# Attention prologue: where the second step's scores are issued

## The chip, the cores and the metric

The kernel runs on one NeuronCore of one Trainium2 chip. The metric is the device time of one execution in microseconds, as the median of several executions. The profile shows the engines of this core: PE (TensorE matmul) with PEld (its weight loads), DVE (VectorE), ACT (ScalarE), POOL (GpSimd) and SP (SyncE, which issues most transfers here).

## What is computed

The reference runs two trunk layers on 1024 latent tokens and 128 context tokens of width 1024, in float32. Layer 0 projects the normalised tokens into a convolution path, a neighbourhood-attention path (8 heads of 64) and a SiLU gate for each. Layer 1 is a pooling mixer. Only the end of layer 0's projections and the start of its attention matter here:

```
a, b, ga, q, k, v, gb = split(h @ w_in)
z_conv = conformer_conv(a, b) * silu(ga)
s = concat(q @ k_window.T * scale + bias, q @ k_ctx.T * scale)
p = softmax(s)
z_att = (p @ concat(v_window, v_ctx)) * silu(gb)
x = x + gate * (concat(z_conv, z_att) @ w_out)
```

## The kernel before

**Projections.** Tokens lie in three groups of 384 (index `g`; the third holds 256 latent and 128 context tokens). A projection is a chain of 24 matmuls into one PSUM bank (`chain_ws`, line 230): eight slices of the inner dimension, with three products each, since each float32 operand is split into a high and a low part. The matmuls of slices 0 to 3 read the first pair of weight tiles, those of slices 4 to 7 the second.

The last projection is `p_ga` (line 764): for each group four chains, `i` = 0 to 3. Chains 0 and 1 read the weights `W0`, chains 2 and 3 read `W1`. Behind each chain stand a Tanh on ACT (line 535) and a product on DVE (line 536, these two are `silu2`), which free the chain's bank, and a second product on DVE (line 774). Below, "chain 0" to "chain 3" are those of the third group, `g` = 2; chain 3 is the last projection chain of the layer.

**Attention.** It runs in 16 steps (`STEPS`, line 1044). Step s is a triple of head pair, half of the grid rows and first column block; steps 0 and 1 share the head pair and the half. The work of one step:

- `scores` (line 939): for each of two column blocks (`matmuls(i)`), six matmuls into two PSUM banks (line 954), then two DVE instructions (line 959) that add the bias, write the tile `p` and take the row extremum. With that four banks are written and four line 959 instructions issued per step. `exp` (line 966): four Exp on ACT with row sums. `norm` (line 968): a reciprocal on DVE and two scalings on POOL (line 972) per column block.
- `turn` (line 976): four groups of four transposes of `p` into banks, which ACT (lines 1137 and 1143) and DVE (line 1144) copy out to `pt`.
- `values` (line 981): 32 matmuls of `pt` with the values, in the step after.

`attention_steps` runs these as a pipeline: in iteration s it issues the scores of step s + 1, the values of step s - 1, the turns of step s, and a part of `prep` (line 875), which turns the queries and keys of the next head pair, or of `prompt_attention`. In iteration 0 the part of `prep` is the two `q_half` calls (transposes at line 891, an ACT copy at line 882 and a DVE subtraction at line 883 each).

`first_scores` (line 1059) issues the scores, exps and norms of step 0 from inside `p_ga`, after chain 2. `attention_ahead(1)` (line 1046), behind the second group, issues the whole `prep` of head pair 0, the second half's bias loads and the values' loads.

**What sets the order.** `attention` wraps its steps in `manual_schedule` (line 1073) for PE, ACT and DVE: there each of the three engines takes these instructions in the order of the program text. For everything else a planner fixes every engine's order ahead of the run, in a time of its own. At each point it takes, of the instructions whose inputs and buffers are there, the one that stands first in the program text. An instruction of `attention` stands behind all of `p_ga` in the text. The finished order is static: on the chip each engine's list is worked off as it stands, each instruction with its waits.

**Buffers that the steps share.**

- PSUM: the tag `mm` has four banks, used by the chains and by the scores. `tp` and `cv` have two banks each, used by the turns and by `prep`.
- Tag `whi`: four tiles. They hold the high parts of the weights and also the tiles `p` of the scores, two for each step. While `p_ga` runs, `W0` and `W1` hold two each.
- Slots 8 to 11 hold the third group's tokens for the chains. Slot 8 becomes half of the values of head pair 0 (`VS`, line 816), slots 10 and 11 the queries of head pair 1 (`QS`, line 814).

Of the kernel before, what the change touches and what calls it, by code (L numbers as in the profile page):

```python
# [46 lines left out]
def _body(tc, nc, A, O, const, wp, arena, tmpp, smp, psp):  # L47
# [3 lines left out]
    def nm(s):  # L51
        uid[0] += 1
        return f"{s}_{uid[0]}"
# [4 lines left out]
    def bank(tag):  # L58
        return psp.tile([P, 512], F32, tag=tag, bufs={"mm": 4, "tp": 2, "cv": 2}[tag], name=nm(tag))

    def tmp(name="t"):
        return tmpp.tile([P, 512], F32, tag="t", name=nm(name))

    def small(n=16, name="sm"):
        t = smp.tile([P, 16], F32, tag="sm", name=nm(name))
        return t[:, :n]
# [68 lines left out]
    V = const.tile([P, NV], F32, name="V")  # L135
# [90 lines left out]
    def chain_ws(out, units, c0, hs, g, nk=8, ks=None):  # L226

        for k in ks or range(nk):
            for i, (a, b) in enumerate(((0, 0), (0, 1), (1, 0))):
                te.matmul(out, wsl(units, a, k, c0, P), hsl(hs, b, k, g), start=(k == 0 and i == 0), stop=(k == nk - 1 and i == 2))  # L230
# [11 lines left out]
    def bg(ns):  # L242

        owed[0] += ns
        i = 0
        while owed[0] > 0 and i < len(streams):
            v = next(streams[i], 0)
            if v == 0:
                del streams[i]
            elif v is None:  # L250
                i += 1
            else:
                owed[0] -= v
        owed[0] = min(owed[0], 0.0)

    def bg_until(cond):
        while streams and not cond():
            if next(streams[0], 0) == 0:
                del streams[0]
# [272 lines left out]
    def silu2(ps, out, n=G):  # L532

        th = tmp("th")
        se.activation(th[:, :n], ps, AF.Tanh, scale=0.5)  # L535
        ve.scalar_tensor_tensor(out, th[:, :n], 1.0, ps, ALU.add, ALU.mult)
# [227 lines left out]
    def p_ga(W0, W1):  # L764
        for g in range(3):
            for i in range(4):
                b = bank("mm")
                chain_ws(b[:, :G], (W0, W1)[i // 2], (i % 2) * P, h0, g)
                bg(1500)
                bg_until(lambda: len(normed) > g)  # L770
                t2 = tmp("t2")
                silu2(b[:, :G], t2[:, :G])
                z = zc[g][:, i, :]
                ve.tensor_tensor(z, z, t2[:, :G], ALU.mult)
                if g == 2 and i == 2:
                    first_scores()
            attention_ahead(g)


# [32 lines left out]
    hold = {}  # L812
# [126 lines left out]
    def scores(step):  # L939


        pr, hf, j0 = step
        qh, ql, kh, kl, _ = qkT[pr]
        o = 0 if hf == 0 else 512
        ps, sts = [], []

        def matmuls(i):
            j = j0 + i
            bs = [bank("mm"), bank("mm")]
            qo = slice(hf * 512 + j * P, hf * 512 + (j + 1) * P)  # L950
            for n, (q, k) in enumerate(((qh, kh), (qh, kl), (ql, kh))):
                for e in range(2):
                    kv = k[H[e], o : o + 1024].rearrange("p (r c) -> p r c", c=64)[:, :, CB[j] : CB[j] + 32]
                    te.matmul(bs[e].rearrange("p (r c) -> p r c", c=32), q[H[e], qo], kv, start=(n == 0), stop=(n == 2))  # L954
            ps.append(wp.tile([P, 2, 512], F32, tag="whi", bufs=4, name=nm("p")))
            sts.append(small(8, "st"))
            for e in range(2):

                ve.tensor_tensor_reduce(
                    out=ps[i][:, e, :], in0=bs[e], in1=bias[hf, e][:, JT[j], :], scale=-1.0, scalar=3e38, op0=ALU.add, op1=ALU.min,  # L960
                    accum_out=sts[i][:, e : e + 1],
                )

        def exp(i, e):
            p, st = ps[i][:, e, :], sts[i]
            se.activation(p, p, AF.Exp, bias=st[:, e : e + 1], scale=-1.0, accum_out=st[:, 2 + e : 3 + e])

        def norm(i):
            st = sts[i]
            ve.reciprocal(st[:, 4:6], st[:, 2:4])  # L970
            for e in range(2):
                gp.tensor_scalar(ps[i][:, e, :], ps[i][:, e, :], st[:, 4 + e : 5 + e], 0.0, ALU.mult, ALU.add)  # L972

        return matmuls, exp, norm, ps
# [69 lines left out]
    STEPS = [(pr, hf, j0) for pr in range(4) for hf in range(2) for j0 in (0, 2)]  # L1044

    def attention_ahead(g):

        if g == 0:
            bias_init(0)
            bias_load(0, 0)  # L1050
        elif g == 1:
            for piece in prep(0):
                piece("cv")()
            bias_init(1)
            bias_load(0, 1)
            with tc.issue_after(last["ck"]):
                hold["V"] = v_load(0)

    def first_scores():

        mm, ex, norm, ps = hold["S"] = scores(STEPS[0])
        for i in range(2):
            mm(i)
            for e in range(2):
                ex(i, e)
            norm(i)
# [9 lines left out]
    def attention_steps():  # L1076

        nonlocal gr  # L1080
        n = len(STEPS)
        sc_, vw, pts = {0: hold["S"]}, {0: hold["V"]}, {}
        right = load_right(0, (13, 15, 17, 2, 3, 4))
        for s in range(n + 1):
            i, pr = s % 4, s // 4
            nxt = None
            if s + 1 < n:
                nxt = sc_[s + 1] = scores(STEPS[s + 1])
                nxt[0](0)
                nxt[0](1)  # L1090
                if pr < 3 and i in (0, 2):
                    bias_load(pr + 1, i // 2)
            if i == 0 and pr < 4:
                pieces = prep(pr + 1) if pr < 3 else []
                prompt = prompt_attention(pr)

                if pr < 3:
                    work = (pieces[0], pieces[2], pieces[4], None), (None, None, None, prompt[1]), (pieces[1], pieces[3], prompt[0], prompt[2])
                else:
                    work = (None,) * 4, (None, prompt[1], None, None), (prompt[0], prompt[2], None, None)  # L1100
            if s == n - 2:
                zs_part(0, 0)
            if s == n - 1:
                zs_part(0, 1)
                zs_part(1, 0)
                zs_part(1, 1)
            if s == n:
                out0_ahead(1)
                units[L0_AT] = [split(*r) for r in raws[L0_AT]]
            if nxt:  # L1110
                nxt[1](0, 0)
            a = work[0][i]("cv") if s < n and work[0][i] else None
            gate = values(STEPS[s - 1], pts.pop(s - 1), vw[STEPS[s - 1][0]]) if s else None
            if nxt:
                nxt[1](0, 1)
                nxt[1](1, 0)
            if a:
                a()
            if nxt:
                nxt[2](0)  # L1120
            if gate:
                gate()
            if n - 4 <= s < n:
                next(right)
            if s < n and work[1][i]:
                work[1][i]("cv")()
            if s == n - 1:
                out0_ahead(0)
            if s == n:
                break  # L1130
            ps = sc_.pop(s)[3]
            pt = pts[s] = new_pt()
            tbs = [bank("tp"), bank("tp"), bank("cv")]
            for x in range(3):
                turn(tbs[x], ps[x // 2][:, x % 2, :])
            for x in range(2):
                se.copy(pt[0][:, x, :], tbs[x])
            if nxt:
                nxt[1](1, 1)
            b = work[2][i]("tp") if work[2][i] else None  # L1140
            tb = bank("tp")
            turn(tb, ps[1][:, 1, :])
            se.copy(pt[1][:, 0, :], tbs[2])
            ve.tensor_copy(pt[1][:, 1, :], tb)
            if nxt:
                nxt[2](1)
            if b:
                b()
            if i == 2 and pr < 3:
                vw[pr + 1] = v_load(pr + 1)  # L1150
            if n - 6 <= s < n - 1:
                hold["R"] = next(right)
            if s == n - 3:
                gr = gr_tile()
                hold["gate"] = load_gates(0)
                y_of(0)
                y_of(1)
            if s == n - 2:
                raws[L0_AT] = load_raw(items[L0_AT][0])
# [80 lines left out]
    def out0_ahead(t):  # L1240

        first_out[t] = out_right(zs0[t], hold["R"])
# [237 lines left out]
```

## Time and profile before

| | us |
|---|---|
| median of three runs | 967.62 (967.46 to 968.0) |
| the profiled execution | 967.13 |
| its span on the core | 965.4 |
| PE busy in the span | 940.7 |
| last projection chain (chain 3) ends | 427.4 |
| scores of step 2 begin on PE | 434.0 |

All positions below are microseconds from the start of the profiled span. The profiled execution took 0.49 us less than the median, and 1.7 us of it lie outside the span. "Busy" counts the time in which an engine has an instruction under way. An engine's idle time matters only where it lies on the chain that sets the end.

### The profile page before, as it was taken

What the parts mean: (1) busy time and instruction counts of PE and PEld (TensorE: products, weight loads), DVE (VectorE), ACT (ScalarE), POOL (GpSimd) and SP (SyncE); (2) the same over time, 40 slices, a digit from 0 to 9 for tenths busy, and PEclk for the clock granted to TensorE, in tenths of its full rate; (3) what the DMA queues carried; (4) which work ended last, traced back from release to release, by engine and by line L of the source; (5) the groups of instructions that cost most, each with busy time, mean ns of one, the idle gap of its engine ahead of it and who ended that gap; (6) DMA issues with size and microseconds to landing.
All of it is one profiled execution on the core that took longest, in us unless ns stands there. A gap on an engine that the chain in (4) does not pass through costs nothing.

```text
span 965.4 us, 16658 instructions
## 1 busy us (share of the span) xinstructions
PE 940.7 (97%) x6388; PEld 863.5 (89%) x6388; DVE 602.5 (62%) x1243; ACT 403.8 (42%) x815; POOL 368.7 (38%) x485
## 2 busy tenths in 40 slices
PE   4899999999999999999999999999999999999998
PEld 2799999899999999987777888899999999998887
DVE  3659999999683444457778547656335455585332
ACT  4365667675611344248886323353222222231010
POOL 2354879999944201124456246430000000004331
PEclk9999999999999999999999999999999999999999
DMA  9956955426111111135344413241110011133311
GB/s 310 301 202 142 352 197 185 154 67 230 48 47 48 47 45 44 43 100 144 116 122 149 151 44 119 98 145 44 55 41 30 30 44 55 66 117 124 109 66 66
DMA packets 87531, 108.53 MB, mean 112 GB/s; under 512 B 10701, under 2 KB 73037, under 8 KB 87340
## 3 DMA queue, kind: packets, MB, share of 16 engines
q1 hardware_dynamic: 82539, 95.93, 31.2%
q0 software_dynamic: 2576, 9.18, 2.4%
q10 hardware_dynamic: 2336, 2.36, 0.7%
q8 instruction: 50, 0.82, 0.4%
q14 instruction: 30, 0.24, 0.1%
HBM read 94.64 MB, written 21.57 MB: 120 GB/s over the span
## 4 chain that ended last, share of the span: by engine, by line
PE 81%; POOL 8%; DMA 5%; ACT 2%; DVE 2%; issue 1%; SPq 1%; DVEq 0%; ACTq 0%; POOLq 0%
PE mm L230 38%; PE mm L1216 10%; PE mm L1209 10%; PE mm L237 8%; POOL zc L555 7%; PE cv L987 3%; DMA wada<-in_w_ada 3%; PE tp L978 2%; PE mm L954 2%; PE mm L1379 2%; PE tp L445 1%; DMA raw<-in_w_in 1%; DMA raw<-in_w_out 1%; PE tp L360 1%; DMA wad<-in_w_ada 1%
## 5 line engine op out<-in xcount | busy, mean ns | idle before, releaser
L230 PE MATMUL mm<-h,whi 128*128 128x384 f32 x1504 | 388.0, 338 | 1.0 <-POOL h L452 0.4
L230 PEld LDWEIGHTS mm<-h,whi 128*128 128x128 f32 x1504 | 271.3, 188 | 4.4 <-issue 1.7
L230 PE MATMUL mm<-h,wlo 128*128 128x384 f32 x752 | 252.4, 336 | 0.0
L555 POOL TENSOR_TENSOR zc<-zc,gr 128x384 f32<-128x384 f32 x138 | 148.8, 1079 | 31.2 <-ACT gr L553 22.8
L237 PE MATMUL mm<-whi,h 128*128 128x256 f32 x864 | 156.8, 284 | 0.6 <-DVE qk L731 0.6
L230 PEld LDWEIGHTS mm<-h,wlo 128*128 128x128 f32 x752 | 141.6, 188 | 0.0
L237 PEld LDWEIGHTS mm<-whi,h 128*128 128x128 f32 x864 | 135.1, 192 | 2.7 <-issue 0.7
L237 PE MATMUL mm<-wlo,h 128*128 128x256 f32 x432 | 122.3, 283 | 0.0
L187 DVE TENSOR_TENSOR wlo<-raw,whi 128x1024 fp32r<-128x1024 f32 (+1 forms) x56 | 68.2, 1219 | 46.8 <-ACT whi L186 46.5
L566 DVE SCALAR_TENSOR_TENSOR cv<-u,convw,cv 128x384 f32<-128x384 f32 (+2 forms) x208 | 94.8, 511 | 0.8
L1216 PE MATMUL mm<-wrh,zs 128*128 128x512 f32 x288 | 92.3, 392 | 0.4 <-POOL wrh L1183 0.4
L1209 PE MATMUL mm<-whi,zs 128*128 128x512 f32 (+1 forms) x304 | 92.5, 379 | 0.0
L186 ACT CAST whi<-raw 128x1024 fp32r<-128x1024 f32 (+1 forms) x56 | 56.9, 1018 | 64.4 <-PE mm L230 25.4
L237 PEld LDWEIGHTS mm<-wlo,h 128*128 128x128 f32 x432 | 82.9, 192 | 0.0
L1223 POOL TENSOR_TENSOR y<-y,og 128x512 f32<-128x512 f32 x34 | 48.6, 1430 | 83.2 <-DVE og L1221 80.1
L553 ACT ACTIVATE gr<-u,convw 128x384 f32<-128x384 f32 (+2 forms) x128 | 64.5, 531 | 29.5 <-POOL zc L555 29.0
L972 POOL TENSOR_SCALAR p<-p,st 128x512 f32<-128x512 f32 x64 | 47.9, 760 | 46.5 <-DVE st L970 30.6
L1209 PEld LDWEIGHTS mm<-whi,zs 128*128 128x128 f32 x304 | 56.0, 188 | 10.6 <-ACT whi L186 0.2
L1216 PEld LDWEIGHTS mm<-wrh,zs 128*128 128x128 f32 x288 | 53.9, 188 | 12.0 <-POOL wrh L1183 0.8
L1221 DVE TENSOR_TENSOR og<-mm,gr 128x512 f32<-128x512 f32 x34 | 23.3, 687 | 59.3 <-PE mm L1216 34.3
L535 ACT ACTIVATE th<-mm 128x384 f32<-128x384 f32 x48 | 23.5, 489 | 81.7 <-PE mm L230 81.6
L1209 PE MATMUL mm<-wlo,zs 128*128 128x512 f32 (+1 forms) x152 | 57.2, 378 | 0.0
(215 smaller groups left out, 1393.3 us busy)
## 6 DMA issues: line engine op xcount, KB each, us to landing
raw<-in_w_in SPq DMA_DIRECT2D x28, 512.0 KB
wad<-in_w_ada SPq DMA_DIRECT2D x16, 768.0 KB
wada<-in_w_ada SPq DMA_DIRECT2D x16, 512.0 KB
raw<-in_w_in SPq DMA_DIRECT2D x32, 256.0 KB
raw<-in_w_out SPq DMA_DIRECT2D x16, 512.0 KB
y0scr<-y POOLq DMA_DIRECT2D x9, 512.0 KB, 3.1
y<-y0scr SPq DMA_DIRECT2D x9, 512.0 KB
x<-in_x_sample SPq DMA_DIRECT2D x8, 512.0 KB
```

Source lines behind the costliest of these rows:

```text
L186: se.copy(hi[:, :n], raw[:, :n])
L187: ve.tensor_tensor(lo[:, :n], raw[:, :n], f(hi[:, :n]), ALU.subtract)
L230: te.matmul(out, wsl(units, a, k, c0, P), hsl(hs, b, k, g), start=(k == 0 and i == 0), stop=(k == nk - 1 and i == 2))
L237: te.matmul(out, hsl(hs, p, k, g, a, P), wsl(units, q, k, 0, 256), start=(k == 0 and i == 0), stop=(k == 7 and i == 2))
L553: se.activation(pr[:, o : o + n], src, AF.Copy, scale=w)
L555: gp.tensor_tensor(z, z, pr, ALU.add)
L566: ve.scalar_tensor_tensor(zp if k == 30 else acc, src, convw[:, c, k : k + 1], zp if k == NPTS[c] else acc, ALU.mult, ALU.add)
L972: gp.tensor_scalar(ps[i][:, e, :], ps[i][:, e, :], st[:, 4 + e : 5 + e], 0.0, ALU.mult, ALU.add)
L987: te.matmul(ob[64 * e : 64 * e + 64, i * P : (i + 1) * P], vw[j0 + i][x][:, 64 * e : 64 * e + 64], pts[i][:, e, n * P : (n + 1) * P], star ...
L1209: te.matmul(b[:, c0 : c0 + n], zs[p][:, k, :], WL[k // 2][q][:, k % 2, c0 : c0 + n], start=(k == 0 and i == 0), stop=(k == 7 and i == 2))
L1216: te.matmul(b, zs[p][:, k, :], WR[q][k // 3][:, k % 3, :], start=(k == 0 and i == 0), stop=(k == 7 and i == 2))
L1223: gp.tensor_tensor(yv, yv, t, ALU.add)
```

## The change

`first_scores` takes the step as an argument. In the third group it is called after chain 1 for step 0 (before: after chain 2) and after chain 2 for step 1 (before: iteration 0 of `attention_steps` issued step 1's scores, exps and norms, under the manual order). Iteration 0 of the attention then issues no scores; the bias loads for the next head pair stay where they were in that iteration. The number of instructions of each kind is the same.

```diff
                 z = zc[g][:, i, :]
                 ve.tensor_tensor(z, z, t2[:, :G], ALU.mult)
-                if g == 2 and i == 2:
-                    first_scores()
+                if g == 2 and i in (1, 2):
+                    first_scores(i - 1)
             attention_ahead(g)
...
-    def first_scores():
+    def first_scores(s):
 
-        mm, ex, norm, ps = hold["S"] = scores(STEPS[0])
+        mm, ex, norm, ps = hold["S", s] = scores(STEPS[s])
...
-        sc_, vw, pts = {0: hold["S"]}, {0: hold["V"]}, {}
+        sc_, vw, pts = {s: hold["S", s] for s in range(2)}, {0: hold["V"]}, {}
...
             if s + 1 < n:
-                nxt = sc_[s + 1] = scores(STEPS[s + 1])
-                nxt[0](0)
-                nxt[0](1)
+                if s:
+                    nxt = sc_[s + 1] = scores(STEPS[s + 1])
+                    nxt[0](0)
+                    nxt[0](1)
                 if pr < 3 and i in (0, 2):
                     bias_load(pr + 1, i // 2)
```

In iteration 0 `nxt` is now None, and the calls `nxt[1]` and `nxt[2]`, each behind `if nxt:`, fall away there.

## Prediction

> **What bounds the kernel now.** I read the page first, for the bounding engine, then the busy times by stretch around the place of the change, then the chain of waits and the timelines there.
>
> ```profile
> PE 940.7 (97%) x6388; PEld 863.5 (89%) x6388; DVE 602.5 (62%) x1243; ACT 403.8 (42%) x815; POOL 368.7 (38%) x485
> PE 81%; POOL 8%; DMA 5%; ACT 2%; DVE 2%; issue 1%; SPq 1%; DVEq 0%; ACTq 0%; POOLq 0%
> ```
>
> PE is busy for 97% and carries 81% of the chain that ended last. The change removes no PE work, so it can win only PE's pauses. Between the end of chain 1 and the scores of step 2 these are (length of a stretch, then busy time by engine; below them pieces of the chain of waits and PE's timeline):
>
> ```profile
> core 0: us, PE busy (x) PEld busy (x) DVE busy (x) ACT busy (x) POOL busy (x), PEclk, DMA share, GB/s
> 416.09:420.59 4.50, 4.50 (x29) 4.22 (x28) 2.06 (x5) 0.86 (x2) 0.83 (x2) 1.00 0.44 118
> 420.59:422.94 2.35, 2.12 (x12) 1.43 (x12) 1.77 (x5) 0.51 (x2) 0.00 (x0) 1.00 0.00 0
> 422.94:427.40 4.46, 4.46 (x26) 4.21 (x26) 2.02 (x8) 2.92 (x8) 2.43 (x4) 1.00 0.15 41
> 427.40:432.83 5.43, 4.00 (x29) 2.80 (x29) 4.20 (x12) 3.93 (x10) 0.74 (x2) 1.00 0.44 127
> 434.00:440.60 6.60, 6.60 (x71) 5.32 (x70) 4.97 (x15) 5.51 (x14) 2.72 (x4) 1.00 0.24 71
> ```
>
> ```profile
> 428.61 0.98 PE mm L954 x4
> 429.59 0.60 PE cv L891 x4
> 430.21 0.69 ACT q L882
> 430.90 1.41 ACT p L966 x4
> 432.30 0.48 ACT pt L1137
> 432.83 0.66 PE tp L891 x4
> 433.48 0.55 PE tp L978 x4
> 434.03 1.62 PE mm L954 x12
> ```
>
> ```profile
> 405.81 1.03 PE L891 MATMUL cv<-ident,qk 128*128 128x128 f32 x8
> 411.72 1.04 PE L898 MATMUL cv<-ident,qk 128*128 128x128 f32 x8
> 417.35 0.27 PE L911 MATMUL cv<-ident,qc 128*128 128x128 f32 x1
> 420.50 2.21 PE L954 MATMUL mm<-k,q 64*128 64x512 f32 x12
> 422.94 0.62 PE L230 MATMUL mm<-h,whi 128*128 128x384 f32 x2 [0.23 <-DVE st L959]
> 430.01 1.04 PE L978 MATMUL tp<-ident,p 128*128 128x128 f32 x8
> 430.88 0.60 PE L978 MATMUL cv<-ident,p 128*128 128x128 f32 x4
> 432.83 0.66 PE L891 MATMUL tp<-ident,qk 128*128 128x128 f32 x4 [1.34 <-ACT pt L1137]
> ```
>
> The stretches are chain 2, step 0's scores, chain 3, and iteration 0 of the attention up to its second group of query transposes; from 434.0 on PE is busy for 6.60 of 6.60 us. Twelve unhindered score matmuls take 1.62. Step 0's took 2.35: 0.73 lost. The 5.43 hold step 1's scores (1.62), four query transposes (0.60) and three turns (430.01 to 431.48, 1.47), which is 3.69 of work: 1.74 lost. So some **2.5 us** of pauses are all that can be won.
>
> **The change part by part.** It moves, for step 1, twelve matmuls, four line 959 instructions, four Exp, two reciprocals and four POOL scalings from iteration 0 to a place ahead of chain 3, and step 0's set from behind chain 2 to behind chain 1. It moves no transfer. The rows that price this are from DVE's, then ACT's, POOL's and SP's timelines, and from the tile view of the values:
>
> ```profile
> 418.06 0.42 DVE L919 TENSOR_TENSOR k<-cv,k 128x256 fp32r<-128x256 f32 x1 [0.28 <-ACT k L915]
> 422.20 0.68 DVE L959 CUSTOM_DVE_ANT_0 p<-mm,bias 128x512 f32<-128x512 f32 x1
> 424.64 0.16 DVE L970 RECIPROCAL st<-st 128x2 f32<-128x2 f32 x1
> 428.47 0.68 DVE L959 CUSTOM_DVE_ANT_0 p<-mm,bias 128x512 f32<-128x512 f32 x1
> 429.08 0.56 DVE L774 TENSOR_TENSOR zc<-zc,t 128x384 f32<-128x384 f32 x1
> ```
>
> ```profile
> 397.69 0.49 ACT L535 ACTIVATE th<-mm 128x384 f32<-128x384 f32 x1 [3.67 <-PE mm L230]
> 401.85 0.49 ACT L535 ACTIVATE th<-mm 128x384 f32<-128x384 f32 x1 [3.67 <-PE mm L230]
> 422.92 0.73 ACT L966 ACTIVATE p<-p,st 128x512 f32<-128x512 f32 x1 [1.82 <-DVE st L959]
> 423.55 0.18 ACT L966 ACTIVATION_READ_ACCUMULATOR p<-p,st 128x1 f32 x1
> ```
>
> ```profile
> 424.97 2.71 POOL L972 TENSOR_SCALAR p<-p,st 128x512 f32<-128x512 f32 x4 [5.99 <-DVE st L970]
> ```
>
> ```profile
> 425.33 0.37 SPq L866 DMA_DIRECT2D vw<-vwin  x1
> ```
>
> ```profile
> L987 PE MATMUL cv<-pt,vw x64: 272/273/325, 442.7 to 457.2; 128*64 128x128 f32 x64
> ```
>
> *A wait that the change adds.* Step 1's line 959 instructions write two `p` tiles of the tag `whi`. Its four tiles are then held by step 0's `p` and by `W1`, which chain 3 still has to read. Step 1's matmuls fill all four `mm` banks, and chain 3, later in the text, gets one only when a line 959 instruction of step 1 has emptied it. By the text's order each would wait for the other. The way out that I see is that the first two turns of step 0, instructions of the attention, go ahead of chain 3: they free step 0's first `p` tile, step 1's evictions begin, a bank comes free, chain 3 starts. That the planner lets attention work pass projection work shows at 428.47 and 429.08: step 1's first line 959 of the attention runs before chain 3's line 774. So I expect on PE: chain 2 with step 0's scores in it, step 1's scores, four query transposes, two or three turns, **then chain 3**, then the second query transposes, the fourth turn and step 2. Chain 3 waits for step 0's whole softmax. The work that it lets past is the 3.69 us that followed it before, so the exchange itself costs nothing; what counts are the pauses before and after chain 3.
>
> *When chain 3 starts.* Step 0's scores need the last key pieces (line 919, done 418.5). In the planner's order they lie later: it put prep's stages 5.9 and 5.6 us apart (405.81, 411.72, 417.35). The last stage, 256 columns wide where the others have 512, gets half of that, some 2.8: 420.0. Bounds are 418.5, when the data are there, and 420.5, where they ran before. I take 420.0, nearer to the planner's spacing. Then:
>
> - six matmuls, half of 1.62: first eviction at 420.85;
> - from it to the first `p` normalised: before, from 422.20 to 424.97 plus half of POOL's 2.71, which is 4.13. Chain 2's Tanh (0.49) may now stand among the Exps; I take half of it: 425.2;
> - the second turn's four transposes behind it, 0.55: 425.8;
> - step 1's first eviction, 0.68 and its hand-over (422.20 to 422.94): 426.5.
>
> Until then PE has chain 2, both score sets and the query transposes: 4.50 + 1.62 + 1.62 + 0.60 from 416.1 is 424.4. So it pauses about a microsecond, turns taken off.
>
> *After chain 3.* It takes 4.16 (the distance of two Tanh, 397.69 to 401.85) to 4.46; with 4.3 it ends at 430.8. The query copy (line 882) heads ACT's manual list; it writes slot 10, which chain 3 reads to the end. Behind it wait the turns' copies (line 1137), and PE's second query transposes wait for the bank that these free. Tanh 0.5, query copy 0.6, first copy 0.55 make 1.65; transposes and fourth turn, 432.83 to 434.03, are 1.2. Step 2's scores start 2.9 later, at 433.7, against 434.03 before: **-0.3 us**. Step 1's evictions, Exps and norms run beside chain 3, where ACT and DVE have room: a chain's stretch holds 2.0 to 2.9 us of either.
>
> *What is priced at nothing.* The values' second half (425.33) waits on SP for slot 8, which chain 3's first half frees, now 3.5 us later; the context keys and bias loads queue behind it. The first matmuls on it come at 442.7, so there are 17 us of cover; without it, 3.5 us would be lost. Bounds for the whole stretch: the whole 2.5 gained, or 2.2 lost in the slow rival below.
>
> Time: the profiled execution, 967.13, stands 0.49 under the median 967.62. The difference -0.3 lies within the span, and as PE has no pause from 434.0 on for many steps it carries through: 966.8 for that execution, 967.3 on the median.
>
> *A rule against it.* The Trainium skill (TensorE: Matmul & The Clock Gate, section on HAM oscillation) asks for no PE pauses over about 3.4 us, since the array then falls back to half its clock. No run here shows that: the longest PE pause in these rows is 1.34 us and the granted clock is 1.00 in each.
>
> **The rivals.**
>
> - **Faster.** Chain 3 gets a bank at once, behind both score sets: 416.1 + 4.50 + 3.24 + 4.16 is 428.0; the 0.60, 1.47 and 1.20 of attention work put step 2 at 431.3, -2.7 us: 964.9. For it: PE's pauses are all waits on DVE and ACT. Against: the four banks, and the row at 422.94, where chain 3 already waited for an eviction of an earlier step's scores.
> - **Slower.** Step 1's second pair of Exps goes ahead of chain 3's Tanh, the query copy and the turns' copies. Exp with its read is 0.91, so +1.8; a third turn ahead of chain 3 that waits for the second norm adds 0.7. From -0.3 that is +2.2: 969.8. It decides as soon as the planner finds these evictions ready before chain 3's end but their Exps still undone. Against: ACT is free beside the chain.
> - **Nothing moves.** The planner leaves step 1 behind chain 3, as before: 967.6.
> - **The clock.** Should the softmax be so late that PE's clock halves, chain 3's 4.2 us double: 971.5.
>
> **How the numbers follow.** Forecast 0.50, nothing 0.13, faster 0.17, slower 0.18, clock 0.02. Measurement tells some 0.2%, 1.9 us, from no change: faster 0.17, same 0.63, slower 0.20. The bounds of the start (-1.5, +0.5) and of the tail put the forecast between 965.7 and 968.6; reaching most of the way to both outer cases gives 965.2 to 969.9.
>
> **What would show it.** PE's timeline: step 0's turns ahead of chain 3, and chain 3 released by a line 959 of step 1; chain 3 near 426.5 to 430.8; step 2's scores at 433.7; the second query transposes waiting for line 1137. If turns follow chain 3, the faster case or none holds. A step 2 later than 435.9 means the slow rival. If step 2 is where I put it and the time still differs by over 1 us, the planner's order changed elsewhere, which I count as no part of this.

## The result and the profile after

The changed kernel is slower by 0.14%: 968.64 us against 967.69 for the kernel before, medians of 22 runs each; the ratio is 1.0014 (95% interval 1.0008 to 1.0020). The predicted 967.3 missed the side: -0.3 us was forecast against the median known then, and +0.95 came. The time lies inside the range given.

A row of the changed kernel's page, PE's part in the chain that ended last:

```profile
PE 76%; POOL 9%; DMA 4%; DVE 3%; ACT 3%; issue 2%; SPq 0%; DVEq 0%; ACTq 0%; POOLq 0%
```

The span on the core is 966.0 us, and PE's busy time is the same 940.7 us. The stretches from the end of chain 1 to step 2's scores, in the columns that stand with the same view above:

```profile
415.64:418.72 3.08, 2.62 (x20) 1.66 (x18) 2.54 (x8) 0.78 (x3) 0.82 (x2) 1.00 0.58 157
418.72:423.08 4.36, 4.36 (x24) 4.11 (x24) 2.02 (x8) 2.91 (x8) 2.34 (x4) 1.00 0.00 0
423.08:427.07 3.99, 3.99 (x26) 2.82 (x25) 2.25 (x5) 0.89 (x2) 0.39 (x1) 1.00 0.01 4
427.07:431.55 4.48, 4.46 (x25) 4.13 (x24) 1.65 (x7) 2.63 (x8) 1.37 (x2) 1.00 0.13 32
431.55:434.32 2.77, 1.10 (x9) 0.84 (x10) 1.94 (x4) 2.45 (x6) 1.36 (x2) 1.00 1.08 298
```

They are: the last key transposes, four query transposes and step 0's scores; chain 2; step 1's scores with three turns; chain 3; and what lies between chain 3 and step 2. PE's timeline shows the instructions in them (start, length, line, count, and in brackets what ended an idle time):

```profile
415.79 0.60 PE L891 MATMUL cv<-ident,qk 128*128 128x128 f32 x4
416.47 1.87 PE L954 MATMUL mm<-k,q 64*128 64x512 f32 x12
418.72 0.62 PE L230 MATMUL mm<-h,whi 128*128 128x384 f32 x2 [0.38 <-DVE st L959]
...
423.08 1.68 PE L954 MATMUL mm<-k,q 64*128 64x512 f32 x9
424.70 1.09 PE L978 MATMUL tp<-ident,p 128*128 128x128 f32 x8
425.63 0.60 PE L978 MATMUL cv<-ident,p 128*128 128x128 f32 x4
426.16 0.98 PE L954 MATMUL mm<-k,q 64*128 64x512 f32 x3
427.07 0.62 PE L230 MATMUL mm<-h,whi 128*128 128x384 f32 x2
...
433.22 0.66 PE L891 MATMUL tp<-ident,qk 128*128 128x128 f32 x4 [1.70 <-ACT pt L1138]
434.32 1.69 PE L954 MATMUL mm<-k,q 64*128 64x512 f32 x12
```

The reader is to see three things. The turns of step 0 (424.70) do stand ahead of chain 3 (427.07), as predicted. Step 1's twelve score matmuls come in two pieces, nine and three, with the turns between. And the pause behind chain 3, 1.70 us for the turns' copies, is there. At 427.07 no wait is named: chain 3 starts as soon as PE is done with what stands ahead of it.

To compare runs with each other I use two distances within one profiled execution, both from the start of chain 1's Tanh: **D2** to step 2's first score matmul, **D3** to step 3's. The rows for D3, before and after (the Tanh of chain 1 in ACT's timeline, step 3's scores in PE's):

```profile
416.11 0.49 ACT L535 ACTIVATE th<-mm 128x384 f32<-128x384 f32 x1 [2.49 <-PE mm L230]
440.57 1.69 PE L954 MATMUL mm<-k,q 64*128 64x512 f32 x12
```

```profile
415.66 0.49 ACT L535 ACTIVATE th<-mm 128x384 f32<-128x384 f32 x1 [2.49 <-PE mm L230]
440.89 1.69 PE L954 MATMUL mm<-k,q 64*128 64x512 f32 x12
```

D3 is 24.46 before and 25.23 after: 0.77 of the 0.95 us has arisen by step 3. Over the steps that follow it neither grows nor shrinks: the first output matmul is 0.73 later.

### The profile page after: what moved, and what is told of

Read it like the earlier page. It is cut to its first block, busy times and chain, and to the rows that moved or that the text cites. A ratio compares the mean times of both kernels' runs of the same rounds, so it can differ in the third digit from the quotient of the medians.

```text
span 966.0 us, 16660 instructions
## 1 busy us (share of the span) xinstructions
PE 940.7 (97%) x6388; PEld 863.7 (89%) x6388; DVE 602.3 (62%) x1243; ACT 403.9 (42%) x815; POOL 369.0 (38%) x485
## 4 chain that ended last, share of the span: by engine, by line
PE 76%; POOL 9%; DMA 4%; DVE 3%; ACT 3%; issue 2%; SPq 0%; DVEq 0%; ACTq 0%; POOLq 0%
PE mm L230 33%; PE mm L1217 10%; PE mm L1210 10%; PE mm L237 8%; POOL zc L555 8%; PE cv L987 3%; PE tp L978 2%; PE mm L954 2%; PE mm L1380 2%; DMA tbias<-in_rpb 1%; DMA texp<-tbias 1%; DMA gb<-in_b_ada 1%; PE tp L445 1%; PE cv L230 1%; ACT gr L553 1%
```

## The experiments

| kernel | D2 | D3 | time, us | before in the same group, us | ratio (95% interval) |
|---|---|---|---|---|---|
| before | 17.85 | 24.46 | | | |
| changed | 18.66 | 25.23 | 968.64 | 967.69 | 1.0014 (1.0008 to 1.0020) |
| own p tiles | 18.66 | 25.23 | 967.73 | 966.68 | 1.0011 (1.0002 to 1.0020) |
| late query copies | 17.03 | 25.87 | 968.18 | 966.68 | 1.0017 (1.0008 to 1.0025) |
| both of these | 17.10 | 25.06 | 967.37 | 966.68 | 1.0005 (0.9996 to 1.0014) |
| step 0 early alone | 18.24 | 24.85 | 967.05 | 966.68 | 1.0002 (0.9993 to 1.0011) |
| paired | 18.16 | 24.72 | 967.36 | 966.72 | 1.0009 (1.0000 to 1.0018) |
| step 1 ahead alone | 19.08 | 25.65 | 968.90 | 966.72 | 1.0023 (1.0014 to 1.0032) |
| step 1 behind chain 3 | 16.21 | 22.79 | 965.14 | 966.72 | 0.9984 (0.9975 to 0.9993) |
| the same again | 16.22 | 22.82 | 964.57 | 966.95 | 0.9975 (0.9966 to 0.9984) |
| step 1 behind, paired | 15.74 | 22.46 | 964.79 | 966.95 | 0.9979 (0.9970 to 0.9988) |
| copies first | 16.47 | 24.34 | 966.51 | 966.72 | 0.9999 (0.9990 to 1.0008) |
| step 0 in the middle | 19.07 | 25.64 | 968.62 | 966.95 | 1.0021 (1.0012 to 1.0030) |
| the same, paired | 19.07 | 25.65 | 968.21 | 966.95 | 1.0015 (1.0006 to 1.0023) |

In most rows the difference in D3 and the difference in time agree within about half a microsecond, so that the cause is to be sought between chain 1 and step 3; the worst are "step 1 ahead alone", off by 1.0, and the repeat of "step 1 behind chain 3", off by 0.7.

D2 alone misleads in three rows (late query copies, both of these, copies first), and DVE shows why. In all 14 profiled executions step 3's first score matmul starts 5.17 to 5.20 us behind step 2's first eviction, that is its first line 959 instruction. In eleven of them this eviction starts 1.37 to 1.52 behind step 2's first score matmul, so that D2 and D3 move together. In those three rows it starts 2.69 to 3.66 behind it: the scores come early and wait for DVE.

**1. Own p tiles for step 1.** Does chain 3 pay for the shared `whi` tiles?

```diff
-            ps.append(wp.tile([P, 2, 512], F32, tag="whi", bufs=4, name=nm("p")))
+            ps.append(wp.tile([P, 2, 512], F32, tag=tag, bufs=bufs, name=nm("p")))
...
-        mm, ex, norm, ps = hold["S", s] = scores(STEPS[s])
+        mm, ex, norm, ps = hold["S", s] = scores(STEPS[s], *(("raw", 2) if s else ("whi", 4)))
```

> The changed kernel, but step 1's two p tiles lie in the two raw-weight buffers, which are idle then, so its evictions need neither W1 nor step 0's p tiles. Measure: the distance from chain 1's Tanh to step 2's first score matmul, 17.85 us before (416.11 to 433.96) and 18.66 after the change (415.66 to 434.32). Theory A (the evictions of step 1 wait for step 0's turns, and chain 3 for the evictions): step 1's first eviction follows its scores instead of the turns, chain 3 starts 0.6 to 0.9 us earlier, distance 17.8 to 18.1, and the time is that of the kernel before within 0.3 us. Theory B (the loss lies in a changed order elsewhere): distance may shrink, but the time stays 0.8 to 1.0 us above before. Theory C (the loss is the early step 0, which waits for the last key pieces): distance stays 18.6.

The wait went and nothing was gained. In DVE's timeline of this kernel step 1's first eviction no longer follows the turns, yet PE's timeline is that of the changed kernel, shifted by 0.4:

```profile
424.64 0.68 DVE L959 CUSTOM_DVE_ANT_0 p<-mm,bias 128x512 f32<-128x512 f32 x1
```

```profile
423.47 1.68 PE L954 MATMUL mm<-k,q 64*128 64x512 f32 x9
425.09 1.09 PE L978 MATMUL tp<-ident,p 128*128 128x128 f32 x8
426.02 0.60 PE L978 MATMUL cv<-ident,p 128*128 128x128 f32 x4
426.55 0.98 PE L954 MATMUL mm<-k,q 64*128 64x512 f32 x3
427.45 0.62 PE L230 MATMUL mm<-h,whi 128*128 128x384 f32 x2
```

In the changed kernel the eviction started at 425.94, 1.24 us behind the turns' start; here 0.45 ahead of it. Chain 3 stays 11.4 us behind the Tanh, and D2 stays 18.66, as theory C had it. Theory A falls for the time ahead of chain 3: PE does not wait there for step 1's eviction. Nor do the shared tiles put the turns ahead of chain 3: without the sharing the planner's order is the same. What fills 423.47 to 427.45 are matmuls. Read from start to next start, nine score matmuls take 1.62 us, as long as twelve do at 433.96 in the kernel before, and three more take 0.90. The single starts in the trace of the changed kernel explain it: two matmuls each at 423.08, 423.42 and 423.66, then one each at 423.90, 424.13 and 424.37, and behind the turns one each at 426.16, 426.50 and 426.74. By the program text a column block's six matmuls alternate between the two heads, each head on one half of the array's rows and with a bank of its own. So the first block ran in pairs, and of the second block one head ran alone, then the other. On average a pair takes 0.27 and so does a single one of the first piece. This became theory P.

**2. Late query copies.** Does the pause behind chain 3 cost what it shows?

```diff
-            a = work[0][i]("cv") if s < n and work[0][i] else None
+            a = work[0][i]("cv") if 0 < s < n and work[0][i] else None
...
                 se.copy(pt[0][:, x, :], tbs[x])
+            if not s:
+                work[0][0]("cv")()
```

> The changed kernel, but in iteration 0 of the attention the first query copies are issued behind the copies of the first two turns, so ACT's list is not headed by a copy that has to wait for chain 3 to leave slot 10. Theory A: the 1.6 us pause between chain 3 and step 2's scores goes; the second query transposes and the fourth turn stand ahead of chain 3 and cost up to 1.2 us there; distance 17.0 to 17.8, time 0.0 to 0.8 us below before. Theory B: time stays 0.8 to 1.0 us above before. Theory C: the distance shrinks only by what C leaves, to 18.0 or more.

The pause went: step 2's scores start with chain 3's end, D2 is 1.63 shorter. But D3 is 0.64 longer than in the changed kernel. In iteration 1, PE's timeline of this kernel has a new wait; DVE's and POOL's timelines show what it is:

```profile
440.06 0.63 PE L978 MATMUL cv<-ident,p 128*128 128x128 f32 x4 [1.22 <-DVE st L970]
```

```profile
436.06 0.74 DVE L883 SCALAR_TENSOR_TENSOR q<-tp,vq,q 128x512 fp32r<-128x512 f32 x1
436.72 0.68 DVE L959 CUSTOM_DVE_ANT_0 p<-mm,bias 128x512 f32<-128x512 f32 x1
439.16 0.75 DVE L883 SCALAR_TENSOR_TENSOR k<-cv,V,k 128x512 fp32r<-128x512 f32 x1
439.83 0.15 DVE L970 RECIPROCAL st<-st 128x2 f32<-128x2 f32 x1
```

```profile
431.66 1.37 POOL L972 TENSOR_SCALAR p<-p,st 128x512 f32<-128x512 f32 x2 [1.36 <-DVE st L970]
```

Step 1's third turn does not wait for its own softmax, whose last scalings on POOL end at 433.03; the reciprocal at 439.83, which the row names, is step 2's. By the program text the turn takes the bank that the key subtraction (439.16, line 883) reads last, and that ends at 439.91. The subtraction stands in DVE's list behind step 2's four evictions, and these (436.72) behind the second query subtraction (436.06).

The loss itself comes from chain 3. The second query transposes and the fourth turn now stand ahead of it, and its Tanh starts 17.20 behind chain 1's instead of 15.96. The query copies have to wait for chain 3's end, and step 2's first eviction for the query subtractions: it starts 3.49 behind chain 3's Tanh, where it took 4.07. So 1.24 were lost ahead of chain 3 and 0.58 won behind it. A pause was moved, with interest.

**3. Both edits.**

> Both edits: own p tiles for step 1 and the late query copies. Theory A: both pauses go, distance 16.2 to 17.0, time 0.9 to 1.6 us below before. Theory B: as in the others, time above before. Theory C: distance not under 17.4.

D2 is 17.10, hardly less than with the late copies alone, and D3 25.06: again a wait comes back in iteration 1, as 0.92 us at the same turn. Chain 3's Tanh starts 16.39 behind chain 1's and step 2's first eviction 3.50 behind that, as with the late copies alone. The expected gain under the kernel before did not come.

**4. Step 0 early, alone.** The kernel before with step 0's call behind chain 1.

```diff
-                if g == 2 and i == 2:
+                if g == 2 and i == 1:
                     first_scores()
```

> Half of the change alone: step 0's scores behind chain 1, step 1's left in iteration 0 of the attention as before. Theory A: chain 3 is not held, the distance is 17.3 to 17.9 and the time that of before within 0.5 us. Theory C: step 0's early scores wait for the last key pieces and the distance is 18.3 to 18.7, as in the full change. Theory B: the time differs from before by more than the distance does.

D3 grows by 0.39, between the two theories. PE's timeline names two waits that the kernel before does not have there:

```profile
416.40 1.87 PE L954 MATMUL mm<-k,q 64*128 64x512 f32 x12 [0.52 <-ACT k L915]
418.65 0.62 PE L230 MATMUL mm<-h,whi 128*128 128x384 f32 x2 [0.38 <-DVE st L959]
```

Step 0 waits for the last key pieces, and chain 2, now behind it in the list, for its first eviction. Against that stand 0.23 for an eviction before chain 3 and a set that is no longer split. In time the difference cannot be told from none.

**5. Paired.** The changed kernel with each score matmul tied behind its partner of the other head.

```diff
+                    with ExitStack() as after:
+                        if tied and prev is not None:
+                            after.enter_context(tc.issue_after(prev))
-                    te.matmul(bs[e].rearrange("p (r c) -> p r c", c=32), q[H[e], qo], kv, start=(n == 0), stop=(n == 2))
+                        m = te.matmul(bs[e].rearrange("p (r c) -> p r c", c=32), q[H[e], qo], kv, start=(n == 0), stop=(n == 2))
+                    prev = m.ins
```

> The changed kernel, with the six score matmuls of a column block issued in pairs (one for each half of the array's rows) for steps 0 and 1: none may pass its partner. D3 is the distance from chain 1's Tanh to step 3's first score matmul: 24.46 us before (416.11 to 440.57), 25.23 after the change, and in the first four runs time and D3 differ from before by the same amount within 0.3 us. Theory P (pairs: in the changed kernel step 1's last bank comes late, so three matmuls of each half run alone at 0.27 us each, the price of a pair; the set costs 2.5 us instead of 1.62): chain 3 starts 0.5 to 0.7 us earlier, D3 24.5 to 24.8, time 0.0 to 0.4 us above before. Theory O (it is the order alone, with the turns ahead of chain 3): D3 stays 25.1 to 25.3, time 0.7 to 1.0 us above.

PE's timeline (line 954 has become 958, 978 983 and 959 964):

```profile
423.38 1.21 PE L958 MATMUL mm<-k,q 64*128 64x512 f32 x7
424.52 1.09 PE L983 MATMUL tp<-ident,p 128*128 128x128 f32 x8
425.45 0.60 PE L983 MATMUL cv<-ident,p 128*128 128x128 f32 x4
425.99 0.97 PE L958 MATMUL mm<-k,q 64*128 64x512 f32 x5
426.89 0.62 PE L230 MATMUL mm<-h,whi 128*128 128x384 f32 x2
```

The set takes 1.14 + 0.90 = 2.04 instead of 1.62 + 0.91 = 2.53, chain 3 starts 10.93 behind the Tanh instead of 11.41, and D3 is 0.51 shorter. The turns still stand ahead of chain 3. Theory P holds and theory O falls for this half microsecond of D3. In time the two kernels, 1.0009 and 1.0014 of before, cannot be told apart.

**6. Step 1 ahead of chain 3, alone.** Step 0 stays behind chain 2.

```diff
-                if g == 2 and i in (1, 2):
-                    first_scores(i - 1)
+                if g == 2 and i == 2:
+                    first_scores(0)
+                    first_scores(1)
```

> The other half of the change alone: step 0's scores stay behind chain 2, and step 1's follow them, still ahead of chain 3. Theory H (chain 3 is held by step 0's softmax as soon as that is late): step 0's first eviction stays 6.1 us behind chain 1's Tanh, its first p tile is normalised 4.1 later, turned 0.6 later, step 1's eviction and its last matmuls take 1.5 more; chain 3 starts at 12.0 to 12.6 behind the Tanh (11.4 in the changed kernel, 6.8 before), D3 25.8 to 26.4, time 1.3 to 2.0 us above before. Theory N (only PE's order counts, the softmax is never late): chain 3 at 11.0 to 11.5, D3 25.0 to 25.3.

This is the dearest order in time (1.0023), with D3 25.65. Here the chain that the prediction had drawn does bind (pieces of the chain of waits; line 960 is the eviction, 979 the turns):

```profile
425.59 0.62 PE tp L979 x4
426.24 0.67 PE tp L979 x4
426.93 0.02 DVEq L960
427.04 0.69 DVE p L960
427.73 0.02 DVE st L960
427.79 2.21 PE mm L230 x11
```

Turns, eviction, chain 3: it starts 11.84 behind the Tanh, a little under the 12.0 expected. So the early step 0 of the full change is no loss beside an early step 1: it pulls the softmax out of the way.

**7. Step 1 behind chain 3.** Both calls one chain later, so that chain 3 is not held, while step 1's scores leave the manual order as they do in the change.

```diff
-                if g == 2 and i in (1, 2):
-                    first_scores(i - 1)
+                if g == 2 and i in (2, 3):
+                    first_scores(i - 2)
```

> Step 0's scores behind chain 2 as before; step 1's behind chain 3, outside the manual order, so that chain 3 is not held and only ACT's and PE's order of iteration 0 is left to the planner. Theory M (the manual order had put the turns' copies ahead of step 1's last Exp; the planner puts all four Exps ahead): step 2's scores 0.9 to 1.4 us later than before, D3 25.2 to 25.9, time 0.8 to 1.4 us above before. If the manual order is worth nothing: D3 24.3 to 24.7 and the time of before.

> The unpaired kernel with step 1 behind chain 3 once more, beside the paired one on the same chip: time 1.2 to 2.0 us below before, D3 22.7 to 22.9.

Theory M was wrong, and this kernel beats both others, twice: 0.9984 and 0.9975 of the time before. The second time it gained 2.4 us, more than the 1.2 to 2.0 expected, with the same D3 within 0.03. Its PE timeline, with ACT's row for the copies behind it:

```profile
419.90 0.60 PE L891 MATMUL cv<-ident,qk 128*128 128x128 f32 x4
420.43 1.77 PE L954 MATMUL mm<-k,q 64*128 64x512 f32 x12
422.43 0.44 PE L230 MATMUL mm<-h,whi 128*128 128x384 f32 x1 [0.23 <-DVE st L959]
426.80 1.68 PE L954 MATMUL mm<-k,q 64*128 64x512 f32 x9
428.42 1.09 PE L978 MATMUL tp<-ident,p 128*128 128x128 f32 x8
429.35 0.60 PE L978 MATMUL cv<-ident,p 128*128 128x128 f32 x4
429.88 0.98 PE L954 MATMUL mm<-k,q 64*128 64x512 f32 x3
430.79 0.65 PE L891 MATMUL tp<-ident,qk 128*128 128x128 f32 x4
```

```profile
429.41 1.05 ACT L1138 COPY pt<-tp 128x512 f32<-128x512 f32 x2
```

Chain 3 starts where it did before, 6.8 behind the Tanh (422.43 - 415.60). The first query transposes stand ahead of it, in a gap that the eviction leaves anyway. Behind it PE works on through scores and turns while ACT does Tanh, query copy, one Exp and the turns' copies; the second query transposes (430.79) find their bank free. In the changed kernel the same PE work stood ahead of chain 3, and nothing was left to cover ACT behind it. Of the 1.64 by which D2 is shorter than before, 1.34 are the pause and 0.49 the query transposes, against 0.32 more for step 1's set (2.53 instead of 2.21); the rest is spread. And the gain reaches D3, since step 2's first eviction starts 1.41 behind its scores, as in the kernel before (1.43).

**8. Step 1 behind chain 3, paired.** The same with step 1's set tied.

> The faster kernel of the second group (step 1's scores behind chain 3, outside the manual order) with step 1's score matmuls issued in pairs. Theory P: the set costs PE 2.0 to 2.1 us instead of 2.5, and nothing else waits behind chain 3, so step 3's scores come 0.3 to 0.5 us earlier: D3 22.3 to 22.5 (22.79 unpaired, 24.46 before), time 1.8 to 2.2 us below before. If the copies of the turns become the limit: D3 stays 22.7 to 22.9.

D3 falls by 0.33 to 22.46, as theory P has it; in time (0.9979) this cannot be told from the unpaired kernel.

**9. Copies first.** The kernel before, its manual order kept, with the first two turns' copies ahead of step 1's second and third Exp in iteration 0.

```diff
-            if nxt:
+            if nxt and s:
                 nxt[1](0, 1)
                 nxt[1](1, 0)
...
                 se.copy(pt[0][:, x, :], tbs[x])
+            if nxt and not s:
+                nxt[1](0, 1)
+                nxt[1](1, 0)
             if nxt:
                 nxt[1](1, 1)
```

(The first column block's `nxt[2](0)` moves behind them in iteration 0.)

> The kernel before, with one change in the manual order of iteration 0: the copies of the first two turns stand ahead of step 1's second and third Exp instead of behind them. Theory: PE's pause of 1.34 us ahead of the second query transposes is a wait for these copies, so it goes; step 1's softmax ends up to 1.1 us later, and its turns in iteration 1 have some 1.7 us to spare. D3 23.2 to 23.7, time 0.7 to 1.2 us below before. If the turns of step 1 then wait: D3 24.0 or more and the time that of before.

D2 shortens by 1.38 and D3 by 0.12, and the time is that of before: step 2's first eviction starts 2.69 behind its scores instead of 1.43. The second query subtraction stands ahead of it on DVE, and this waits for the second query copy on ACT, which has three Exps ahead of it now and starts 17.77 behind chain 1's Tanh, where it started 17.76 behind before. The third turn of step 1 waits as in experiment 2 (PE's timeline); its own softmax had ended at 436.09.

```profile
438.38 0.63 PE L978 MATMUL cv<-ident,p 128*128 128x128 f32 x4 [0.52 <-DVE st L970]
```

**10 and 11. Step 0 in the middle of chain 2**, where the prediction had put it: `chain_ws` is called for slices 0 to 4, then `first_scores(0)`, then for slices 5 to 7; once unpaired, once paired.

> The changed kernel, but step 0's scores are called after 15 of chain 2's 24 matmuls, where the prediction had put them, and step 1's behind chain 2. Theory W (behind chain 1 step 0's scores wait 0.52 us for the last key pieces and chain 2 another 0.38 for their first eviction): both waits go, while the set may be split (up to 0.7 more than 1.87). D3 24.5 to 25.0 (25.23 in the changed kernel). If the early place is not what costs: D3 25.2 or more, or the softmax of step 0, now later, holds chain 3 as in s1_ahead: 25.4 to 25.7.

> The same with both steps' score matmuls in pairs. Theories W and P together: D3 24.0 to 24.5 (24.72 paired with step 0 behind chain 1), time within 0.5 us of before. If W falls: D3 24.7 or more.

Neither tests what it was made for. The planner put step 0 behind all of chain 2 in both, with the order of experiment 6, and D3 is that of experiment 6. Theory W could not be tried so. What the pair does show is that pairing buys nothing where the softmax holds chain 3: it starts 11.84 behind the Tanh unpaired and 11.85 paired.

## Why the prediction was wrong

In microseconds behind chain 1's Tanh:

| step of the prediction | predicted | measured |
|---|---|---|
| step 0's first eviction | 4.7 | 2.3 |
| first p tile normalised | 9.1 | 6.5 |
| second turn done | 9.7 | 10.1 |
| chain 3 starts | 10.4 | 11.4 |
| chain 3 ends | 14.7 | 15.9 |
| step 2's scores start | 17.6 | 18.7 |

- **The order was right, the reason given for it was not.** The turns of step 0 pass chain 3, as said. But the prediction derived this from the `p` tiles that step 1 shares with step 0 and `W1`, and experiment 1, without that sharing, has the same order. What puts the turns there is not shown. The change in PE's busy time is nil, as said.
- **The place of step 0 was wrong, to no harm.** It was put inside chain 2 at 420.0; it ran at 416.47, ahead of chain 2. So the softmax, which was to set chain 3's start, was done 2.6 us early. Alone this early place costs 0.39 of D3; in the full change the moved query transposes (415.79) fill the wait for the keys.
- **The step that failed is the wait that was to set chain 3's start.** The prediction had softmax, second turn and step 1's eviction end last, at 10.4, and PE idle for about a microsecond until then. On the chip that eviction ended at 426.63, and chain 3 started at 427.07 without a wait: PE's own list ended last. The prediction had put that list, with three turns, at 4.50 + 1.62 + 1.62 + 0.60 + 1.47, which is 9.8; it took 11.4. That chain 3 is only 1.0 late is partly luck: 0.6 of the overrun fell into the idle time that the prediction had granted PE. Where step 0's scores do stay late, as in experiment 6, the wait that it had drawn does end last, at 11.84.
- **The terms of that list that were mis-sized are the two score sets.** 0.91 of the 1.6 is step 1's set: "The work that it lets past is the 3.69 us that followed it before, so the exchange itself costs nothing" had it at 1.62, and it took 1.62 for nine and 0.91 for three, 2.53, as its second half ran unpaired. 0.63 is step 0's set, which with chain 2's wait of 0.38 for an eviction took 2.25 (416.47 to 418.72) instead of 1.62. Keeping pairs together gives back 0.51 of D3. Chain 3's start, 1.0 late, holds nearly the whole miss of 1.1.
- **The pauses of the kernel before were read too simply.** Of the 0.73 "lost" by step 0's set only 0.23 is a wait; the rest is the set itself, whose second half ran mostly unpaired. Step 1's set was taken at 1.62 there, and it took 2.21 too, from 427.31 to 429.52 (PE's timeline of the kernel before, and DVE's product that frees chain 3's bank). Seven of its matmuls start by 428.12, the other five from 428.61 on, when that bank is free. So the exchange costs 0.32 against the kernel before, not 0.91, and not nothing.

```profile
427.31 2.28 PE L954 MATMUL mm<-k,q 64*128 64x512 f32 x12
429.52 0.66 PE L891 MATMUL cv<-ident,qk 128*128 128x128 f32 x4
```

```profile
428.00 0.55 DVE L536 SCALAR_TENSOR_TENSOR t<-th,mm 128x384 f32<-128x384 f32 x1 [1.95 <-ACT th L535]
```

- **The part behind chain 3 held**: 2.9 predicted, 2.8 measured, with 1.70 of it the wait for line 1138. As rival "slower" had it, Exps of step 1 ran ahead of chain 3's Tanh, but they ended as the chain did and cost under 0.1. (That rival priced an Exp with its read at 0.91 by adding two rows that overlap: in ACT's timeline the Exps of one set start 0.70 to 0.72 apart.)
- **"Faster"** did not happen in this change. The mean granted clock of every run lay between 0.998 and 1.0, so the rival of the halved clock has no support here.
- **The step to the whole time held in size**: 0.77 by step 3, 0.95 in the medians.

Against the kernel before, PE's rows from chain 1's Tanh to step 2's scores add up to the 0.81 of D2: step 1's set +0.32, the pause behind chain 3 +0.36 (1.70 instead of 1.34), the first query transposes with what is left of the wait for the keys +0.19 (0.68 instead of 0.49), the two chains +0.18, step 0's set with the wait behind it -0.19 (2.25 instead of 2.44), and the rest -0.05.

What stays open: why the planner splits step 1's set and puts the turns where it does, and why "step 1 ahead alone" costs a microsecond more in time than in D3. In its profiled execution 0.36 of that arises between step 3 and the last step, whose first score matmul starts 103.92 behind the Tanh against 102.37 before; the rest is not placed.

## What to carry to other kernels

Work that moves ahead of a long chain no longer covers what waits behind that chain: look which latency it hid, as ACT's here, before counting the move as free. A shared buffer can look like the cause of an order and of a wait, and be neither: without it the changed kernel's order and D3 stayed the same. So take the buffer away in an experiment before blaming it. And a pause removed at one place counts only at a point some steps on: two edits that took 1.4 to 1.6 us out of D2 left 0.12 us of it, or a loss, in D3. Look for the instruction that this later point hangs on, here step 2's first eviction on DVE. A wait that a profile names can be that of another step's instruction; compare its time with the end of the work that it seems to belong to.

## What the hardware showed that I had not expected

Score matmuls that use 64 of the array's 128 rows ran two at a time when both halves alternated in the list: twelve in 1.62 us, 0.27 a pair. With one half alone three took 0.90 to 0.91, some 0.3 each, and three behind three pairs 0.27 each. PE reads as fully busy in both cases (3.99 of 3.99 us in the changed kernel), so busy time does not show it; the count of instructions in a stretch does. The Trainium skill (TensorEngine Tiling (Array Packing), sections Theoretical Speedup and Gotcha 1: PSUM Pressure) gives up to 2x for a contraction of 64 or less and says that the row tiles write different PSUM banks; these rows agree with the factor. They also show that a bank which comes late for one half takes the factor away from the other: in the kernel before, step 1's seventh matmul ran alone at 428.12, and its partner came at 428.61, behind the product (428.00 + 0.55) that frees the bank.
